# Third mixer's heads issued one by one, four stick-breaking heads in flight, and the conditioning products dealt out anew over the stages

## The chip, the core and the metric

The kernel runs on one core of a Trainium2 chip. The metric is the device time of the whole kernel in microseconds. The kernel before was timed three times: 1038.05, 1036.2 and 1028.79 us, median 1036.2 us. One more execution was recorded by the profiler; it took 1033.1 us, with 1031.4 us from its first to its last instruction.

## The reference, cut to what matters

Three blocks over 256 tokens of width 1024. Each adds a gated mixer and then a gated convolutional FFN to x. Shifts, scales and gates come from the conditioning vector c through a large weight matrix per block; these products are called conditioning products below.

```python
cond = silu(c)
mod = cond @ ada_w[i] + ada_b[i]                 # 1024 x 6144 for each block
sh1, sc1, g1, sh2, sc2, g2 = split(mod, 6)
h = rms_norm(x, norm_mix[i]) * (1.0 + sc1) + sh1
x = x + g1 * mixer_i(h)
h = rms_norm(x, norm_ffn[i]) * (1.0 + sc2) + sh2
x = x + g2 * conv_ffn(h)

# mixer 0, stick-breaking, 16 heads of 64
z = q @ k.T / 8
log_keep = where(strict, log_sigmoid(-z), 0.0)
suffix = cumsum(log_keep, reverse=True) - log_keep
o = where(strict, exp(log_sigmoid(z) + suffix), 0.0) @ v
...
# mixer 1: sparse attention, 64 selected keys a query
...
# mixer 2: 8 heads of sliding-window attention with sinks beside a 4-head recurrence
p = exp(scores - m) / (sum(exp(scores - m)) + exp(sink - m))     # window 128
f = lb + (1 - lb) * sigmoid(f_logit)
S_t = diag(f_t) S_{t-1} + (1 - f_t) i_t^T;  o_t = S_t^T q_t
x = x + gate * (concat([rms_norm(attn), rms_norm(rec) * silu(g)]) @ w_out)
```

## The kernel before

**Weight products.** All large matrix products are taken in three parts: a weight piece (`raw`, 128x1024) is split into a high part `wh` by ScalarE (`high`, L409) and a low part `wl` by VectorE (`low`, L421), the activations likewise into `xh` and `xl`, and TensorE adds wh·xh, wh·xl and wl·xh (`three`, all recorded at L300). One piece is 24 matmuls with 256 columns. There are 290 pieces, and their splits are made three pieces ahead.

**Stages.** The stages follow each other: 0 `stick` (mixer 0), 1 `ffn(0)`, 2 `sparse`, 3 `ffn(1)`, 4 `mixed` (mixer 2), 5 `ffn(2)`. Between two stages stands a serial piece. `residual` adds the gated product to x, one 128x256 part at a time on VectorE (L691), writes `xh` and `xl` of the un-normalised x (L687), and sums squares (L714). `opening` then takes the first six pieces (144 matmuls) of the next stage with the un-normalised x, while the norm goes TensorE sums `po<-ones,sq`, VectorE and ScalarE `rs` (L656 to L662), TensorE spread `po<-ident,rs`, ScalarE `rbc`, VectorE `xm` (L772). The `wl` of these six pieces stand in VectorE's queue among this work.

**Heads.** A mixer's heads run in the background of the dense work. `heads_in_flight` is a generator, advanced by `post` (which is called once after each piece) `rate` times a piece. It keeps some heads between `scores` (score matmuls, which take a bank of the accumulators `acc`, four in all) and `middle` (for stick-breaking the suffix sums, for window heads the transposes `flip`). With `pair` = 2 heads are started two at a time. Two heads of a pair have 64-row operands in the upper and the lower half of the array, and `chained` binds the order of their matmuls. `product` takes two heads at once. In `output` the heads that are still open are brought to their middle before the output product (`acc<-oh,wh` and its like) begins, and `st["out"]` is then true.

**Conditioning products.** A product is one VectorE instruction (`ada_op`, L532) over a 128x1024 block of weights with a short read of the accumulator behind it. Four make a group, with a small `mod` addition behind it (L558); there are 36 groups. The first 4 groups are done before the first stage is under way. The blocks after the first 16 pass through a ring of three buffers; POOL issues the load of a block (`ada_load`, L525, 512 KB) when the product three blocks earlier has freed its buffer. `post` spreads the products evenly over a stage's pieces so that `TARGETS[i]` groups are reached by the end of stage i. Before the change the six stages take 6, 7, 5, 6, 6 and 2 groups.

**Order.** A scheduler, which simulates the program, fixes the order of each engine's instructions when the kernel is built. On the chip VectorE, ScalarE and POOL take theirs strictly in that order.

**Recurrence.** The third mixer's recurrence (`level_decay`, `level_scores`, `recurrence`, L1554 to L1640) has eight levels, two at a time: TensorE decays `acc<-lev,gth` and `acc<-lev,gtl`, ScalarE exponentials `X`, VectorE products `X` (L1574), TensorE scores `acc<-X` or `mm<-X` with 64 columns, VectorE `COPY_PREDICATED` into `S` (L1595). It ends in `mixed` behind the dense input pieces, and the output product waits for it.

Of the kernel before, what the change touches and what calls it, by code (L numbers as in the profile page):

```python
# [208 lines left out]
SPR = 1  # L209
QUIET = (4,4,4,4,6,4)  # L210
FE = 0
TARGETS = (10,17,22,28,34,36)

IX = (2,2,2,2,0,0,0,0)
DD = (1,)*16
# [55 lines left out]
class Prog:  # L271
# [187 lines left out]
    def post(self):  # L459
        i = sum(e < self.pos for e in self.ends)  # L460
        start, end = self.ends[i - 1] + QUIET2[i] if i else 0, self.ends[i] - QUIET[i]
        if start <= self.pos <= end and i != 2:
            ops = 4 * (TARGETS[i] - self.ada_i) - (4 - len(self.ada_todo) if self.ada_todo else 0)
            self.ada_credit = min(self.ada_credit, 1) + max(0, ops - self.ada_credit) / (end + 1 - self.pos)
# [20 lines left out]
    def heads_in_flight(self, n, st, ready, scores, middle, product, lag=2, pair=1):  # L485

        st.update(hold=False, out=False, done=0, open=0, ready=0, split=0)
        a = c = 0
        ticks = {}
        while st["done"] < n:  # L490
            can = a < n and not st["hold"] and ready(a) and a - c < (3 - pair if st["out"] else 4 - pair)
            did = False
            if st["done"] + 1 < c and (st["done"] % 4 or not st["split"]):
                product(st["done"])
                st["done"] += 2
                did = True
            if c < a and (a - c >= 2 or not can) and self.tick - ticks[c] >= lag and c - st["done"] < WP:
                middle(c)
                c += 1
                did = True  # L500
            if can:
                scores(a)
                for a in range(a, a + pair):
                    ticks[a] = self.tick
                a += 1
                did = True
            st["open"] = a - c
            yield did
# [834 lines left out]
    def mixed(self):  # L1343
        nc, I = self.nc, self.I
        blocks = ((0, slice(0, 128)), (1, slice(128, 384)))
        with ExitStack() as outer:
# [4 lines left out]
            band_r = sk.tile([128, 384], F32R, name="band")  # L1351
# [39 lines left out]
            ka = sk.tile([128, T], F32, name="ka")  # L1391
            va = sk.tile([128, 2, 128], F32, name="va")
            st, part = {}, []
            sp = pool("hgx", 2)
            qa = sp.tile([128, 4, T], F32, name="ro")
# [35 lines left out]
            for half in range(2):  # L1431
                h, l = self.next()
# [10 lines left out]
            def keys():  # L1443
                nc.scalar.activation(ka, bkv[:, 0:T], AF.Identity, bias=self.v("bka"))
                nc.vector.tensor_tensor(va, bkv[:, 256:512].rearrange("p (t c) -> p t c", t=2),
                                        rows[:, None, 512:640].to_broadcast([128, 2, 128]), op=ALU.add)
                self.bg.extend([self.heads_in_flight(8, st, lambda h: True, scores, flip, product, 2, 2), window()])

            Z, E, P, PO = {}, {}, {}, {}

            def scores(h0):
                for h in (h0, h0 + 1):
                    Z[h] = self.bank("acc")
                chain = []
                for t, j in ((1, 1), (1, 0), (0, 1), (0, 0)):
                    r = slice(j * 64, j * 64 + 64)
                    chain.append(self.mmul(Z[h0 + j][:, t * 128:128 + t * 256], qa[r, h0 // 2, t * 128:t * 128 + 128],
                                           ka[r, 0:128 + t * 128], start=t == 1))
                self.chained(chain)
                for h in (h0, h0 + 1):  # L1460
                    self.mmul(Z[h][:, 0:384], self.ident_r, band_r, stop=True)
                    softmax(h)

            def softmax(h):
                i, kv = divmod(h, 2)
                z = Z[h]
                sink = self.v("sink", i + 4 * kv, 1)
                m = sp.tile([128, 4, 2], F32, name="wm", bufs=3)
                e = E[h] = sp.tile([128, 384], F32, name="we", bufs=3)
# [265 lines left out]
```

## Time and profile before

| | before |
|---|---|
| three runs, us | 1038.05, 1036.2, 1028.79 (median 1036.2) |
| the profiled execution, us | 1033.1 |
| its span, us | 1031.4 |
| TensorE matmul busy | 998.2 us, 97% |
| VectorE busy | 833.5 us, 81% |
| ScalarE busy | 636.4 us, 62% |
| POOL busy | 98.9 us, 10% |
| mean granted TensorE clock | 0.979 of full speed |

The span is that of the one core from its first to its last instruction. The matmul busy time counts matmuls that are pipelined and whose ends are modelled, so 97% is no measure of TensorE at its peak: at half the granted clock it reads as busy too. The places to read are therefore the stretches in which the clock is below full or in which TensorE waits for something.

### The profile page before, as it was taken

The numbers are of one execution on the slowest core, as the hardware profiler recorded it, in microseconds if no ns is written. First come the engines' busy times: TensorE is split into PE (matmuls) and PEld (weight loads), VectorE is DVE, ScalarE is ACT, GpSimd is POOL, SyncE is SP. The second block draws the span as 40 slices with busy tenths as digits, with TensorE's granted clock in tenths as the row PEclk, the third lists the DMA queues.
The fourth block names the chain that finished last, engine by engine and source line by source line (L and its number), as shares of the span: only waits on it lengthen the run. The fifth ranks groups of instructions, "written<-read, shape, count | busy, mean of one in ns | idle before, by whom it ended". The sixth has DMA issues, their size and how long they took to land.

```text
span 1031.4 us, 19958 instructions
## 1 busy us (share of the span) xinstructions
PE 998.2 (97%) x7984; PEld 964.1 (93%) x7984; DVE 833.5 (81%) x1550; ACT 636.4 (62%) x1095; POOL 98.9 (10%) x180
## 2 busy tenths in 40 slices
PE   7999989999999999998999999999999999999996
PEld 5998878999999989988999999999899999999996
DVE  6956768999999889987998889897994588566664
ACT  6575647855555684886965555588854378445543
POOL 0015530011111010110000101100120000000000
PEclk9999989999999999999999999999986999999998
DMA  9969764578888476642767777745880336566531
GB/s 362 405 239 336 243 241 159 209 276 300 290 295 289 142 275 216 241 169 83 268 225 268 283 268 284 277 150 210 306 312 21 124 127 226 200 210 220 211 137 42
DMA packets 45647, 235.66 MB, mean 228 GB/s; under 512 B 5361, under 2 KB 5889, under 8 KB 27889
## 3 DMA queue, kind: packets, MB, share of 16 engines
q1 hardware_dynamic: 25922, 164.21, 44.1%
q0 software_dynamic: 19344, 69.78, 19.3%
q8 instruction: 62, 1.02, 0.4%
q10 hardware_dynamic: 288, 0.39, 0.1%
q14 instruction: 31, 0.25, 0.1%
HBM read 233.29 MB, written 1.07 MB: 227 GB/s over the span
## 4 chain that ended last, share of the span: by engine, by line
PE 81%; issue 8%; DVE 5%; DMA 3%; ACT 2%; POOL 1%; DVEq 0%; SPq 0%; POOLq 0%; ACTq 0%
PE acc L300 32%; PE mm L300 29%; PE po L300 10%; PE small L300 10%; DMA adaw<-ada 2%; DVE x L691 1%; DVE xl L687 1%; POOL adaw L525 1%; DVE wl L421 1%; DVE adaw L532 1%; ACT wh L409 0%; DMA x<-xT 0%; DVE sq L714 0%; PE acc L1126 0%; ACT e L330 0%
## 5 line engine op out<-in xcount | busy, mean ns | idle before, releaser
L409 ACT ACTIVATE wh<-raw 128x1024 fp32r<-128x1024 f32 x290 | 304.7, 1057 | 224.8 <-PE acc L300 87.1
L421 DVE TENSOR_TENSOR wl<-raw,wh 128x1024 fp32r<-128x1024 f32 x290 | 353.0, 1223 | 96.1 <-PE acc L300 27.8
L300 PE MATMUL mm<-xh,wh 128*128 128x256 f32 (+1 forms) x872 | 244.5, 285 | 2.1 <-ACT wh L409 2.1
L300 PE MATMUL mm<-xl,wh 128*128 128x256 f32 (+1 forms) x872 | 245.4, 283 | 0.7 <-DVE xl L687 0.7
L300 PE MATMUL mm<-xh,wl 128*128 128x256 f32 (+1 forms) x872 | 244.3, 282 | 0.0
L532 DVE SCALAR_TENSOR_TENSOR adaw<-adaw,cond 128x1024 f32<-128x1024 f32 x144 | 175.2, 1221 | 10.7 <-DMA adaw<-ada 10.4
L300 PEld LDWEIGHTS mm<-xh,wh 128*128 128x128 f32 x872 | 163.5, 189 | 4.9 <-ACT wh L409 2.7
L300 PEld LDWEIGHTS mm<-xl,wh 128*128 128x128 f32 x872 | 164.6, 189 | 2.3 <-DVE xl L687 1.1
L300 PEld LDWEIGHTS mm<-xh,wl 128*128 128x128 f32 x872 | 164.0, 188 | 0.5 <-issue 0.3
L300 PE MATMUL acc<-gh,wl 128*128 128x256 f32 x528 | 149.0, 283 | 0.0
L300 PE MATMUL acc<-gh,wh 128*128 128x256 f32 x528 | 148.1, 282 | 0.0
L300 PE MATMUL acc<-gl,wh 128*128 128x256 f32 x528 | 147.9, 281 | 0.0
L525 POOL DMA_DIRECT2D adaw<-ada x125 | 66.6, 533 | 738.6 <-DVE adaw L532 624.9
L300 PEld LDWEIGHTS acc<-gl,wh 128*128 128x128 f32 x528 | 100.3, 190 | 0.2 <-DVE gl L337 0.2
L300 PEld LDWEIGHTS acc<-gh,wh 128*128 128x128 f32 x528 | 98.8, 188 | 0.0
L300 PEld LDWEIGHTS acc<-gh,wl 128*128 128x128 f32 x528 | 98.8, 187 | 0.0
L300 PE MATMUL small<-xh,wh 128*128 128x256 f32 x240 | 67.6, 282 | 0.0
L300 PE MATMUL small<-xh,wl 128*128 128x256 f32 x240 | 67.5, 281 | 0.0
L300 PE MATMUL small<-xl,wh 128*128 128x256 f32 x240 | 67.3, 281 | 0.0
L300 PE MATMUL acc<-oh,wh 128*128 128x256 f32 x192 | 53.1, 297 | 2.0 <-ACT oh L336 1.5
L300 PE MATMUL acc<-xh,wl 128*128 128x258 f32 (+1 forms) x192 | 52.4, 284 | 2.1 <-DVE wl L421 2.0
L300 PE MATMUL acc<-ol,wh 128*128 128x256 f32 x192 | 53.7, 286 | 0.4 <-DVE ol L337 0.4
(310 smaller groups left out, 2073.9 us busy)
## 6 DMA issues: line engine op xcount, KB each, us to landing
raw<-ffn SPq DMA_DIRECT2D x99, 1024.0 KB, 5.0
adaw<-ada POOLq DMA_DIRECT2D x125, 512.0 KB, 5.2
raw<-dsa SPq DMA_DIRECT2D x15, 1024.0 KB, 6.4
raw<-hg SPq DMA_DIRECT2D x15, 1024.0 KB, 5.9
adaw<-ada SPq DMA_DIRECT2D x19, 512.0 KB, 10.2
raw<-sb SPq DMA_DIRECT2D x16, 512.0 KB, 10.2
raw<-sb SPq DMA_DIRECT2D x8, 1024.0 KB, 8.5
bias<-scr POOLq DMA_DIRECT2D x8, 256.0 KB, 8.3
```

What stands on the lines that cost most here:

```text
L300: return self.nc.tensor.matmul(o, a, b, start=start, stop=stop, skip_group_check=True).ins
L409: inst = nc.scalar.activation(h[:, :k * n], self.raws[b][:, c0:c0 + k * n], AF.Copy).ins
L421: inst = nc.vector.tensor_tensor(l[:, :k * n], self.raws[b][:, c0:c0 + k * n], h[:, :k * n], op=ALU.subtract).ins
L525: self.nc.gpsimd.dma_start(raw, self.I[f"ada{L}"][b])
L532: return self.nc.vector.scalar_tensor_tensor(w, w, 1.0, self.cond[n // 24], op0=ALU.mult, op1=ALU.mult, accum_out=self.M[n // 12][:, n % 1 ...
L687: return lambda: nc.vector.scalar_tensor_tensor(self.xl[:, m, 0:T], self.x[:, m], a, self.xh[:, m, 0:T], op0=ALU.mult, op1=ALU.subtract)
L691: self.lastx = nc.vector.scalar_tensor_tensor(self.x[:, m], o, self.gate(L, h, m), self.x[:, m], op0=ALU.mult, op1=ALU.add).ins
```

## The change

Three edits.

1. `TARGETS` goes from (10,17,22,28,34,36) to (13,20,25,32,34,36). The six stages then take 9, 7, 5, 7, 2 and 2 groups: three groups (12 products, 12 loads) more in stage 0, one more in stage 3, four fewer in stage 4.
2. The limit on heads between scores and middle is 3 in place of 4 - `pair` outside of the output product. For `pair` = 1 it stays 3. For stick-breaking (`pair` = 2) it was 2, so that a pair was started only with at most one head waiting; now one is started with two waiting, which makes four heads.
3. The window heads of the third mixer are started singly (`pair` = 1, `lag` = 2 by default). `scores` of one head is a 128-column matmul, a 256-column matmul and the band; nothing is bound by `chained`. `softmax` becomes part of `scores`; lines below move up by nine.

```diff
-TARGETS = (10,17,22,28,34,36)
+TARGETS = (13,20,25,32,34,36)
...
-            can = a < n and not st["hold"] and ready(a) and a - c < (3 - pair if st["out"] else 4 - pair)
+            can = a < n and not st["hold"] and ready(a) and a - c < ((3 - pair) if st["out"] else 3)
...
-                self.bg.extend([self.heads_in_flight(8, st, lambda h: True, scores, flip, product, 2, 2), window()])
+                self.bg.extend([self.heads_in_flight(8, st, lambda h: True, scores, flip, product), window()])
...
-            def scores(h0):
-                for h in (h0, h0 + 1):
-                    Z[h] = self.bank("acc")
-                chain = []
-                for t, j in ((1, 1), (1, 0), (0, 1), (0, 0)):
-                    r = slice(j * 64, j * 64 + 64)
-                    chain.append(self.mmul(Z[h0 + j][:, t * 128:128 + t * 256], qa[r, h0 // 2, t * 128:t * 128 + 128],
-                                           ka[r, 0:128 + t * 128], start=t == 1))
-                self.chained(chain)
-                for h in (h0, h0 + 1):
-                    self.mmul(Z[h][:, 0:384], self.ident_r, band_r, stop=True)
-                    softmax(h)
-
-            def softmax(h):
+            def scores(h):
                 i, kv = divmod(h, 2)
-                z = Z[h]
+                r = slice(kv * 64, kv * 64 + 64)
+                z = Z[h] = self.bank("acc")
+                self.mmul(z[:, 0:128], qa[r, i, 0:128], ka[r, 0:128], start=True)
+                self.mmul(z[:, 128:384], qa[r, i, 128:256], ka[r, :])
+                self.mmul(z[:, 0:384], self.ident_r, band_r, stop=True)
```

**VectorE, between stage 0 and ffn(0).** The names are those of `residual` and `opening` above. Before, from the first `wl` behind the residual to `xm`:

```order
L421 TENSOR_TENSOR wl<-raw,wh 128x1024
L687 SCALAR_TENSOR_TENSOR xl<-x,gain_173,xh 128x256 x3
L714 TENSOR_TENSOR sq<-sq 128x512
L687 SCALAR_TENSOR_TENSOR xl<-x,gain_173,xh 128x256
L421 TENSOR_TENSOR wl<-raw,wh 128x1024
L714 TENSOR_TENSOR sq<-sq 128x512
L656 TENSOR_SCALAR rs_1725<-po 128x2
L659 SCALAR_TENSOR_TENSOR rs_1725<-rs_1725 128x2
L660 TENSOR_TENSOR rs_1725<-rs_1725 128x2
L662 SCALAR_TENSOR_TENSOR rs_1725<-rs_1725 128x2
L421 TENSOR_TENSOR wl<-raw,wh 128x1024
L772 TENSOR_TENSOR xm<-x,po 128x512 x2
```

Of the change, first from the same `wl` to the second one:

```order
L421 TENSOR_TENSOR wl<-raw,wh 128x1024
L532 SCALAR_TENSOR_TENSOR adaw,mod_170<-adaw,cond_167 128x1024
L687 SCALAR_TENSOR_TENSOR xl<-x,gain_173,xh 128x256 x2
L532 SCALAR_TENSOR_TENSOR adaw,mod_170<-adaw,cond_167 128x1024
L687 SCALAR_TENSOR_TENSOR xl<-x,gain_173,xh 128x256
L714 TENSOR_TENSOR sq<-sq 128x512
L532 SCALAR_TENSOR_TENSOR adaw,mod_170<-adaw,cond_167 128x1024
L687 SCALAR_TENSOR_TENSOR xl<-x,gain_173,xh 128x256
L421 TENSOR_TENSOR wl<-raw,wh 128x1024
```

and then, without a gap, on to `xm`:

```order
L714 TENSOR_TENSOR sq<-sq 128x512
L532 SCALAR_TENSOR_TENSOR adaw,mod_171<-adaw,cond_167 128x1024
L558 TENSOR_TENSOR mod_170<-mod_170,vec 128x4
L532 SCALAR_TENSOR_TENSOR adaw,mod_171<-adaw,cond_167 128x1024
L656 TENSOR_SCALAR rs_1765<-po 128x2
L532 SCALAR_TENSOR_TENSOR adaw,mod_171<-adaw,cond_167 128x1024
L659 SCALAR_TENSOR_TENSOR rs_1765<-rs_1765 128x2
L660 TENSOR_TENSOR rs_1765<-rs_1765 128x2
L662 SCALAR_TENSOR_TENSOR rs_1765<-rs_1765 128x2
L421 TENSOR_TENSOR wl<-raw,wh 128x1024
L532 SCALAR_TENSOR_TENSOR adaw,mod_171<-adaw,cond_167 128x1024
L772 TENSOR_TENSOR xm<-x,po 128x512 x2
```

Seven conditioning products (`adaw`) now stand between that `wl` and `xm`, where none stood, and one more stands ahead of that `wl`, between two `x` additions of the residual: eight between the residual's first `x` and `xm`. Of these, four stand ahead of the last `sq`, two between it and the first `rs`, one between two `rs`, and one ahead of `xm`. A ninth stands just ahead of the first `x`.

**TensorE, window heads of the third mixer.** `ka` and `ro` are the keys and queries of the window heads, `band` the mask, `pT` and `va` the weights and values, `mm` dense work. Before, the third pair (one of its matmuls comes ahead of two heads' product):

```order
L300 MATMUL acc<-ka,ro 128x256
L300 MATMUL mm<-wl,xh 128x256
L300 MATMUL po<-pT,va 64x256 x2
L300 MATMUL po<-pT,va 64x128 x2
L300 MATMUL acc<-ka,ro 128x256
L300 MATMUL acc<-ka,ro 128x128 x2
L300 MATMUL acc<-band,ident_r 128x384 x2
```

Of the change, two single heads behind the first product:

```order
L300 MATMUL po<-pT,va 64x256 x2
L300 MATMUL po<-pT,va 64x128 x2
L300 MATMUL acc<-ka,ro 128x128
L300 MATMUL acc<-ka,ro 128x256
L300 MATMUL acc<-band,ident_r 128x384
L1126 MATMUL acc<-ident,we 128x128 x3
L300 MATMUL acc<-ka,ro 128x128
L300 MATMUL acc<-ka,ro 128x256
L300 MATMUL acc<-band,ident_r 128x384
```

A head's three matmuls now stand together, with another head's transposes between two heads, and no two matmuls of different row halves are neighbours. The first two pairs of before stand undivided, the last two are divided as the one shown.

**VectorE, the recurrence's first levels.** `X` and `S` are the recurrence's. Before:

```order
L532 SCALAR_TENSOR_TENSOR adaw,mod_172<-adaw,cond_168 128x1024
L1574 TENSOR_TENSOR X<-X,kq 128x256 x2
L561 SCALAR_TENSOR_TENSOR gain_175<-mod_172,vec 128x2
L421 TENSOR_TENSOR wl<-raw,wh 128x1024
L1574 TENSOR_TENSOR X<-X,kq 128x256 x4
L532 SCALAR_TENSOR_TENSOR adaw,mod_172<-adaw,cond_168 128x1024
L1574 TENSOR_TENSOR X<-X,kq 128x256 x3
L532 SCALAR_TENSOR_TENSOR adaw,mod_172<-adaw,cond_168 128x1024
L1574 TENSOR_TENSOR X<-X,kq 128x256
L1512 TENSOR_TENSOR sq<-sq 128x512
L532 SCALAR_TENSOR_TENSOR adaw,mod_172<-adaw,cond_168 128x1024
L1574 TENSOR_TENSOR X<-X,kq 128x256
```

and of the change, from the start of `S` to the first copy into it:

```order
L1596 TENSOR_TENSOR S<-acc,ident 128x512 x2
L421 TENSOR_TENSOR wl<-raw,wh 128x1024
L1565 TENSOR_TENSOR X<-X,kq 128x256 x7
L1503 TENSOR_TENSOR sq<-sq 128x512
L1565 TENSOR_TENSOR X<-X,kq 128x256 x3
L421 TENSOR_TENSOR wl<-raw,wh 128x1024
L532 SCALAR_TENSOR_TENSOR adaw,mod_172<-adaw,cond_168 128x1024
L1586 COPY_PREDICATED S<-pick,acc 128x512
```

Between the start of `S` and its last copy stood seven products; one is left, behind a `wl` and right ahead of the first copy.

## Rows read from the trace of the kernel before

**Rows 1.** The page of the profile: the span, and the chain of work that ended last, by engine.

```profile
span 1031.4 us, 19958 instructions
...
PE 81%; issue 8%; DVE 5%; DMA 3%; ACT 2%; POOL 1%; DVEq 0%; SPq 0%; POOLq 0%; ACTq 0%
```

**Rows 2.** Busy time by stretch of the span: start and end in us, length, then for PE, PEld, DVE, ACT and POOL the busy us with the count of instructions, the mean granted clock, the DMA engines' share, and GB/s.

```profile
100.00:151.00 51.00, 44.07 (x320) 37.69 (x319) 36.18 (x69) 25.42 (x55) 24.64 (x42) 0.93 0.76 254
151.00:163.00 12.00, 9.80 (x79) 9.34 (x78) 10.60 (x22) 7.57 (x15) 0.00 (x0) 1.00 0.10 39
163.00:176.00 13.00, 13.00 (x111) 13.00 (x110) 11.03 (x21) 11.46 (x21) 0.00 (x0) 1.00 0.67 238
704.00:756.00 52.00, 50.76 (x414) 47.37 (x414) 46.17 (x101) 42.01 (x97) 8.50 (x16) 1.00 0.75 278
756.00:787.00 31.00, 29.07 (x165) 27.98 (x164) 24.03 (x56) 15.46 (x38) 3.18 (x6) 0.66 0.50 175
787.00:807.00 20.00, 19.37 (x127) 18.84 (x127) 6.33 (x13) 7.29 (x21) 0.00 (x0) 0.76 0.00 1
```

**Rows 3.** The same stretches, with the conditioning products and their loads alone: busy us of DVE (a product and its accumulator read count as two) and of POOL.

```profile
100.00:151.00 51.00, 21.41 (x36) 9.69 (x18) 0.93 0.76 254
151.00:163.00 12.00, 0.00 (x0) 0.00 (x0) 1.00 0.10 39
704.00:756.00 52.00, 20.05 (x33) 8.50 (x16) 1.00 0.75 278
756.00:787.00 31.00, 6.76 (x12) 3.18 (x6) 0.66 0.50 175
```

**Rows 4.** The conditioning products from 99 to 151 us: ns of one (min, median, max), first and last start, shape; what they waited for in us and times; and from issue to landing of a load.

```profile
L532 DVE SCALAR_TENSOR_TENSOR adaw<-adaw,cond x18: 1212/1224/1410, 99.0 to 141.2; 128x1024 f32<-128x1024 f32 x18
L532 DVE DVE_READ_ACCUMULATOR adaw<-adaw,cond x18: 75/80/83, 100.2 to 142.3; 128x1 f32 x18
...
  DMA adaw<-ada: 6.8, 5
...
DMA to landing us min/median/max: 3.8/5.0/7.1
```

**Rows 5.** VectorE in order of time, from the residual of stage 0 through the opening of ffn(0): start, us, line, operation; in brackets the idle time before and what ended it.

```profile
150.97 1.66 DVE L691 SCALAR_TENSOR_TENSOR x<-acc,mod,x 128x256 f32<-128x256 f32 x4 [0.62 <-PE acc L300]
...
160.76 0.68 DVE L714 TENSOR_TENSOR sq<-sq 128x512 f32<-128x512 f32 x1
162.64 0.16 DVE L656 TENSOR_SCALAR rs<-po 128x2 f32<-128x2 f32 x1 [1.21 <-PE po L300]
163.31 0.16 DVE L659 SCALAR_TENSOR_TENSOR rs<-rs 128x2 f32<-128x2 f32 x1 [0.51 <-ACT rs L330]
...
165.40 1.28 DVE L772 TENSOR_TENSOR xm<-x,po 128x512 f32<-128x512 f32 x2 [0.41 <-ACT rbc L749]
...
167.74 1.22 DVE L421 TENSOR_TENSOR wl<-raw,wh 128x1024 fp32r<-128x1024 f32 x1
```

**Rows 6.** TensorE in order of time in the end of stage 0 and the opening of ffn(0).

```profile
138.43 0.87 PE L300 MATMUL po<-a,V 128*64 128x256 f32 x8 [1.58 <-POOL a L1031]
...
143.69 1.22 PE L300 MATMUL mm<-s,nu 128*128 128x256 f32 x2 [0.86 <-POOL s L1031]
...
161.58 1.02 PE L300 MATMUL po<-ones,sq 128*128 128x1 f32 x8 [0.71 <-DVE sq L714]
...
164.34 0.61 PE L300 MATMUL po<-ident,rs 128*128 128x128 f32 x4
...
170.53 0.41 PE L300 MATMUL acc<-xh,wl 128*128 128x258 f32 x2
```

**Rows 7.** TensorE in order of time, window heads of the third mixer: the first pair with its bands and the dense matmul behind them, then the third and the beginning of the fourth pair.

```profile
707.11 0.92 PE L300 MATMUL acc<-ka,ro 64*128 64x256 f32 x8
...
708.42 0.28 PE L300 MATMUL mm<-xh,wh 128*128 128x256 f32 x1
...
726.03 0.70 PE L300 MATMUL acc<-ka,ro 64*128 64x256 f32 x2
...
727.78 0.92 PE L300 MATMUL acc<-ka,ro 64*128 64x256 f32 x6
...
729.08 0.28 PE L300 MATMUL mm<-wh,xl 128*128 128x256 f32 x1
...
732.67 0.70 PE L300 MATMUL acc<-ka,ro 64*128 64x256 f32 x2 [0.76 <-ACT pT L1129]
733.84 0.55 PE L1126 MATMUL acc<-ident,we 128*128 128x128 f32 x3 [0.48 <-ACT we L1485]
```

**Rows 8.** TensorE in order of time, the recurrence.

```profile
764.26 0.66 PE L300 MATMUL acc<-X 128*128 128x64 f32 x4 [0.52 <-DVE X L1574]
765.39 0.39 PE L300 MATMUL acc<-lev,gth 128*128 128x256 f32 x1 [0.47 <-ACT X L330]
...
783.22 3.68 PE L300 MATMUL mm<-X 128*128 128x64 f32 x16 [0.78 <-DVE S L1595]
...
787.71 0.58 PE L300 MATMUL mm<-lev,gth 128*128 128x256 f32 x1
...
789.59 0.32 PE L300 MATMUL acc<-ol,wh 128*128 128x256 f32 x1
...
793.76 6.46 PE L300 MATMUL mm<-X 128*128 128x64 f32 x40 [0.63 <-ACT X L330]
```

## The prediction

> **What bounds the kernel now.** I read the page first. Of a span of 1031.4 us the chain that ended last runs 81% through TensorE, 8% through issue, 5% through VectorE and 3% through DMA [rows 1]. Most stages are dense matmuls, so work that moves there between other engines costs nothing while VectorE keeps up. What can change is where TensorE waits or runs at half its clock, so I went on to the busy times by stretch [rows 2]. Two places stand out. From 100 to 163 us (end of the stick-breaking stage, residual, opening of the first FFN) TensorE is busy 53.9 of 63 us. From 756 to 807 us (the recurrence) it reads as busy, but its granted clock is 0.66 and 0.76 of full. The clock has two levels, 1.2 and 2.4 GHz; 0.66 over 31 us makes 2 x 0.34 x 31 = 21.1 us at the lower, 0.76 over 20 us makes 9.6, together 30.7 us. Next I asked where the conditioning products stand [rows 3]: 18 between 100 and 151 us, none from 151 to 176 us, some 16 from 704 to 756, 6 from 756 to 787.
>
> The change takes products away from the second place and puts them into the first. So the sum is made of these two, and of the window heads.
>
> **Stage 0.** Twelve products more must go through the ring. In the end of this stage the ring is already the pace: a product takes 1.224 us and its accumulator read 0.080, together 1.30, but from the first at 99.0 to the eighteenth at 141.2 they come every 2.48 us, and five times VectorE waited for the load, 5.0 us from issue to landing [rows 4]. Leaving out the two longest steps, where nothing asked for a product, I take 2.43. TensorE's own waits in this stretch (for example 1.58 and 0.86 us [rows 6], both for POOL, which also issues the loads) are what four heads in flight could remove. But by the new order 21 further products stand between the one at 99.0 and the first addition to x: the last of them starts at 99.0 + 21 x 2.43 = 150.0, ends at 151.3, and the addition follows, where it came at 150.97 before [rows 5]. So I count no gain from the fourth head, and +0.4.
>
> Then come the eight products between the first x and xm. All three wl and the norm wait behind them in one queue, so I replay that queue with the durations of [rows 5]. Four products stand ahead of the last sum of squares: 160.76 + 5.2 = 165.96. Two products and a mod addition follow: rs, which came at 162.64 after 1.21 us of idle time, comes at 165.96 + 0.68 + 2.6 + 0.07 = 169.3. The seventh covers ScalarE's 0.51: the second rs is at 170.7 instead of 163.31, +7.4. The spread on TensorE, at 164.34 [rows 6], moves by as much, but four dense matmuls (0.5 us) now stand ahead of it, so TensorE loses 6.9. The eighth covers the 0.41 ahead of xm, which comes at 173.75, and the fourth wl at 176.1 instead of 167.74; it ends at 177.3, and TensorE wants it at 170.53 + 6.9 = 177.4 [rows 6], just in time. The seventh and eighth wait for loads issued after the fourth and fifth: 0.5 of issue, 5.0 of landing and 1.30 of product come to about 1 us more than the queue leaves them. That makes 7.9. It isn't given back: behind the opening TensorE is dense, 13.00 of 13.00 us [rows 2].
>
> TensorE's clock: the drain already lost 0.07 of 51 us, that is 7.1 us at the lower level or 3.6 us of work [rows 2]. In the opening TensorE will now wait four or five times in 15 us. The cost lies between 0 and a second such 3.6; I take 1.0, since TensorE waited there before (9.80 busy of 12 us) at full clock. Stage 0 in all: 0.4 + 7.9 + 1.0 = +9.3. Bounds: if loads land as the quickest did, 3.8 us, the pace is about 2.0, x is bound by TensorE, some 3 us earlier, the extra load wait is gone, and +3.9 is left; with a pace 0.1 us longer, 2 us of load waits and the whole clock loss it is 0.4 + 2.1 + 6.9 + 2.0 + 3.6 = +15.
>
> The Trainium skill, "DMA: Bandwidth & Descriptors", Anatomy of one DMA, fits a load issued by GpSimd as 2.0 us plus bytes at 436 GB/s; as an estimate by that page, 512 KB take 3.2 us. The trace's quickest is 3.8 and its median 5.0, so the trace does not agree under this load, and I go by the trace; by the page the ring would turn in about 1.8 us a product and stage 0 would cost what the lower bound says.
>
> **Other stages.** The group added to stage 3 (four products, 5.2 us of VectorE spread over a whole stage of dense pieces) is hidden by dense matmuls; if VectorE were full there, it would cost those 5.2. The sixteen taken from stage 4 free VectorE between 704 and 756 us, where TensorE is busy 50.76 of 52 us [rows 2]: at most 1.2 us, which I count below.
>
> **Window heads singly.** An undivided pair takes 708.42 - 707.11 = 1.31 us with its bands; a divided one 0.70 at 726.03 and 1.30 from 727.78 to 729.08, 2.0 [rows 7]. A single head has no row; I bound it by half an undivided pair (0.66) and half a divided one (1.0), and take 1.0, since nothing in the other row half runs beside it. Two pairs were undivided: 2 x (2.0 - 1.31) = +1.4; the other two gain nothing. Two waits of the fourth pair (0.76 and 0.48 [rows 7]) come from softmax steps that now start a head earlier: -1.2. Net +0.2, from -1.2 to +1.4.
>
> The Trainium skill, "TensorEngine Tiling (Array Packing)", Theoretical Speedup, promises up to twice the throughput where the contraction is 64 or less, and speaks against this edit. By that rule alone all four pairs would lose, four times 0.7, +2.8. The trace agrees for the undivided pairs only; half of the pairs had been pulled apart by the scheduler already.
>
> **Recurrence.** Six products from 756 to 787 us [rows 3], 1.30 us each, stood between its VectorE steps; one is left. TensorE's waits that lead back to those are 0.52, 0.47 and 0.78, and 0.63 before the last scores [rows 8]; also the eight decay matmuls from 787.71 to 789.59 (1.9 us at half clock), which stood behind the first output matmuls, now stand ahead in time that was waited. That sums to 4.3, and the fewer waits in a row give a little of the clock back: -4.5. The clock decides how much more. All 30.7 us at half clock would shrink by 15.4 if it stayed up; a replay of ScalarE's and VectorE's queues by their durations leaves 13.5 of it. Before the fall at about 766 us TensorE had only waits of 0.5 us or so, and in the new order the first copy into S stands behind a wl and a product (2.5 us), so a wait of 1.5 to 1.9 us stands at the same place. I take it that the clock falls again: -4.5, bounds 0 and -13.5.
>
> **Sum.** 9.3 + 0.2 - 4.5 = +5.0 us against the profiled execution's 1033.1 us, 1038.1. The median of the three runs is 3.1 higher than that execution, which would make 1041; I give 1040. About 1% (10 us) is what a measurement of this kernel can tell from no change.
>
> **Rivals.**
> *The clock stays up in the recurrence.* For it: six products leave, and S starts before the decays. Against: the wait at the first copy. It gives 9.3 + 0.2 - 13.5 = -4.0, 1029 to 1032, and is over 1% faster (the other side) only if stage 0 costs less than 3 us, near its lower bound: 1033.1 + 3 - 13.5 = 1022.6. Chance 0.25, of which 0.1 below 1026.
> *The ring is quick enough.* Loads land in less than 4 us, the stage is bound by its heads, and four in flight save TensorE's waits there. For it: the quickest load, and the DMA share of 0.10 from 151 to 163 us [rows 2]. Against: a share of 0.76 before. It gives 3.9 + 0.2 - 4.5: no change, 1033 to 1036. Chance 0.15. The fit of the Trainium skill's page named above would make this case the likeliest; no load of this ring in the trace was as quick as it says.
> *The clock falls in the opening as well, or the loads are late there.* Stage 0 at +13 to +15, and in the recurrence half the gain: +11 to +13, 1046 to 1050. Chance 0.2.
> *The change does little:* pairs that were mostly divided, and heads that wait for VectorE with or without a fourth; that is part of the sum above and has no price of its own.
>
> **Chances.** Likeliest 0.4, at 1040 with its own range 1035 to 1045; the others as above. The range 1028 to 1051 takes in all but the low end of the first rival and the high end of the third. Faster by over 1%: 0.14; slower by over 1%, above 1046.5: 0.22 (the third rival and the top of the likeliest); within: 0.64.
>
> **What would show it.** In the profile after, eight conditioning products between the first x and xm, xm about 22 us after the first x (it was 14.4), and TensorE waiting 6 to 8 us more there than the 2.2 it did. Products every 2.4 us up to the first x, at about 151. Window heads at 1.0 us each. In the recurrence at most one product, and a granted clock still below full from about 764 us. I am wrong if xm follows x as before, if the drain of the heads ends by 147 us, or if the recurrence's clock reads 1.00.

## The result, and the profile after

The change makes the kernel faster, by little: 1026.05 us in the median of 20 runs (1023.58 to 1028.81) against 1031.8 us of the kernel before in 20 runs (1028.45 to 1038.05). The ratio is 0.9938, 95% interval 0.9924 to 0.9952: 6 us, inside the 1% that was called no change, but of the other sign than forecast and below the stated range. The profiled execution took 1026.6 us, its span is 1024.9 us.

Two things have to be kept apart. The time of before was taken as 1036.2 us, the median of three runs; 20 runs put it at 1031.8. And the sum was made against one profiled execution, whose mean granted clock was 0.979; in the 83 further runs of before that came with the experiments the mean clock lies between 0.971 and 0.989, 0.984 in the median, and the time follows it (correlation 0.85 between a run's time and its time multiplied by one minus its clock). The changed kernel's 20 runs lie between 0.987 and 0.992, 0.990 in the median. A run's time multiplied by its mean clock is 1014.9 us for before and 1015.4 us for the changed kernel, its time multiplied by one minus the clock 16.5 and 10.3 us (medians over the runs; before's are over the 83). So the difference between the kernels is about as large as the difference in what the lower clock took. This is a rough measure, since it counts a low clock as lost also where TensorE would have waited otherwise: in the changed kernel's profile (1 - 0.70) x 22.7 = 6.8 us of it stand between the first addition to x and xm in the first opening, where they cost no time that shows (see the part on stage 0).

Where the two traces differ, stretch by stretch, for the changed kernel. The columns are as in [rows 2].

```profile
100.00:151.00 51.00, 42.74 (x328) 36.82 (x326) 42.78 (x82) 26.11 (x57) 29.47 (x46) 1.00 0.79 276
151.00:163.00 12.00, 8.40 (x53) 7.98 (x53) 12.00 (x25) 6.85 (x13) 1.71 (x4) 0.80 0.60 214
163.00:176.00 13.00, 12.19 (x72) 11.92 (x72) 11.79 (x21) 4.70 (x10) 2.53 (x5) 0.66 0.81 268
704.00:756.00 52.00, 52.00 (x404) 47.46 (x404) 35.29 (x75) 42.41 (x95) 2.12 (x4) 1.00 0.50 181
756.00:787.00 31.00, 30.30 (x259) 29.03 (x258) 25.05 (x52) 21.85 (x54) 1.58 (x3) 1.00 0.44 154
787.00:807.00 20.00, 19.01 (x159) 18.68 (x160) 10.20 (x22) 9.03 (x23) 0.53 (x1) 1.00 0.03 5
```

The clock has changed places. In the recurrence it is 1.00, where [rows 2] had 0.66 and 0.76; from 151 to 176 us it is 0.80 and 0.66, where it had 1.00. VectorE is now full from 151 to 163 us (12.00 of 12).

The opening of the first FFN on VectorE, in order of time, to be read against [rows 5]:

```profile
148.45 1.22 DVE L532 SCALAR_TENSOR_TENSOR adaw<-adaw,cond 128x1024 f32<-128x1024 f32 x1 [1.02 <-DMA adaw<-ada]
...
149.60 1.26 DVE L691 SCALAR_TENSOR_TENSOR x<-acc,mod,x 128x256 f32<-128x256 f32 x3
...
164.04 0.69 DVE L714 TENSOR_TENSOR sq<-sq 128x512 f32<-128x512 f32 x1
164.64 1.22 DVE L532 SCALAR_TENSOR_TENSOR adaw<-adaw,cond 128x1024 f32<-128x1024 f32 x1
...
165.86 1.22 DVE L532 SCALAR_TENSOR_TENSOR adaw<-adaw,cond 128x1024 f32<-128x1024 f32 x1
...
167.00 0.15 DVE L656 TENSOR_SCALAR rs<-po 128x2 f32<-128x2 f32 x1
167.73 1.23 DVE L532 SCALAR_TENSOR_TENSOR adaw<-adaw,cond 128x1024 f32<-128x1024 f32 x1 [0.57 <-DMA adaw<-ada]
...
168.88 0.16 DVE L659 SCALAR_TENSOR_TENSOR rs<-rs 128x2 f32<-128x2 f32 x1
...
170.76 1.22 DVE L532 SCALAR_TENSOR_TENSOR adaw<-adaw,cond 128x1024 f32<-128x1024 f32 x1 [0.20 <-DMA adaw<-ada]
...
172.31 1.28 DVE L772 TENSOR_TENSOR xm<-x,po 128x512 f32<-128x512 f32 x2 [0.32 <-ACT rbc L749]
```

From the first x to xm it is 172.31 - 149.60 = 22.7 us (14.4 before): the eight products stand in the chain, and the idle times of 1.21 and 0.51 us in [rows 5] are gone into them. The first x is 1.4 us earlier than before, right behind the product that starts at 148.45.

The stretches of the whole kernel, from the starts of the first residual addition (x) and the first xm of each stage in the traces, in us:

| stretch | before | after | difference |
|---|---|---|---|
| start to first x of stage 0 | 151.0 | 149.6 | -1.4 |
| that x to xm | 14.4 | 22.7 | +8.3 |
| first FFN, xm to the next x | 177.9 | 177.5 | -0.4 |
| opening, sparse mixer, opening, second FFN | 325.5 | 326.4 | +0.9 |
| opening of the third mixer | 14.0 | 15.5 | +1.5 |
| third mixer, xm to the next x | 141.7 | 126.7 | -15.0 |
| the rest | 207.0 | 206.5 | -0.5 |

In the third mixer the first decay matmul comes 0.9 us later after xm (73.9, was 73.0), from it to the start of the last score matmul it takes 30.6 us (was 44.1), and from there to the x 22.1 (was 24.6).

### The profile page after: what moved, and what is told of

Read it like the earlier page. It is cut to its first block, busy times and chain, and to the rows that moved or that the text cites. A ratio compares the mean times of both kernels' runs of the same rounds, so it can differ in the third digit from the quotient of the medians.

```text
span 1024.9 us, 19967 instructions
## 1 busy us (share of the span) xinstructions
PE 990.4 (97%) x7984; PEld 956.5 (93%) x7984; DVE 833.8 (81%) x1550; ACT 636.5 (62%) x1095; POOL 102.9 (10%) x180
## 4 chain that ended last, share of the span: by engine, by line
PE 87%; DVE 6%; ACT 2%; DMA 2%; issue 1%; POOL 1%; DVEq 0%; SPq 0%; POOLq 0%; ACTq 0%
PE acc L300 34%; PE mm L300 32%; PE po L300 10%; PE small L300 10%; DMA adaw<-ada 2%; DVE adaw L532 1%; DVE x L691 1%; DVE xl L687 1%; DVE wl L421 1%; ACT wh L409 1%; PE acc L1126 1%; DVE sq L714 0%; DMA x<-xT 0%; POOL s L1031 0%; POOL a L1031 0%
## 5 line engine op out<-in xcount | busy, mean ns | idle before, releaser
L421 DVE TENSOR_TENSOR wl<-raw,wh 128x1024 fp32r<-128x1024 f32 x290 | 352.8, 1223 | 103.3 <-PE acc L300 30.6
L300 PE MATMUL acc<-gh,wh 128*128 128x256 f32 x528 | 147.9, 282 | 0.0
L300 PE MATMUL acc<-xh,wh 128*128 128x258 f32 (+1 forms) x192 | 55.6, 298 | 0.0
```

The costliest lines, as they stand in the source:

```text
L300: return self.nc.tensor.matmul(o, a, b, start=start, stop=stop, skip_group_check=True).ins
L421: inst = nc.vector.tensor_tensor(l[:, :k * n], self.raws[b][:, c0:c0 + k * n], h[:, :k * n], op=ALU.subtract).ins
```

## The experiments

The table puts the runs together: the median, the ratio to before with its interval as recorded (not the ratio of the medians shown), the median of the runs' mean clocks (for before: of the 83), and of the profile the first x of stage 0, the stretch from it to xm, the third mixer from xm to x, and the granted clock from 755 to 807 us.

| kernel | us | ratio | clock of the runs | first x | x to xm | mixer | recurrence |
|---|---|---|---|---|---|---|---|
| before (profile shown) | 1031.8 | | 0.984 | 151.0 | 14.4 | 141.7 | 0.70 |
| before again | 1031.68 | 0.9998 (0.997 to 1.0025) | 0.984 | 152.3 | 14.5 | 139.6 | 0.84 |
| the change | 1026.05 | 0.9938 (0.9924 to 0.9952) | 0.990 | 149.6 | 22.7 | 126.7 | 1.00 |
| TARGETS alone | 1029.67 | 0.9987 (0.9966 to 1.0008) | 0.985 | 150.2 | 23.7 | 125.5 | 1.00 |
| single heads alone | 1030.73 | 1.0004 (0.9969 to 1.0039) | 0.985 | 152.2 | 15.3 | 133.1 | 0.97 |
| limit alone | 1025.63 | 0.9951 (0.9928 to 0.9975) | 0.989 | 145.3 | 14.4 | 140.1 | 0.84 |
| both edits on heads | 1026.12 | 0.9925 (0.9892 to 0.9958) | 0.990 | 145.6 | 14.5 | 141.8 | 0.74 |
| change, 10 groups in the first FFN | 1023.8 | 0.9915 (0.9884 to 0.9946) | 0.992 | 145.8 | 14.4 | 127.8 | 0.97 |
| change, groups spread | 1020.78 | 0.9875 (0.9843 to 0.9907) | 0.992 | 147.6 | 14.5 | 129.5 | 0.93 |
| the same again | 1021.18 | 0.9889 (0.985 to 0.9928) | 0.992 | 147.9 | 15.3 | 126.6 | 1.00 |
| spread, one group in stage 0 | 1021.35 | 0.9889 (0.9846 to 0.9933) | 0.992 | 149.5 | 14.5 | 128.2 | 0.97 |
| spread, matmuls added | 1019.9 | 0.987 (0.9818 to 0.9921) | 0.994 | 148.3 | 14.4 | 127.3 | 1.00 |
| before, matmuls added | 1026.18 | 0.9937 (0.991 to 0.9963) | 0.992 | 151.0 | 14.5 | 133.7 | 0.97 |
| change, VectorE operations added | 1030.86 | 0.9982 (0.9956 to 1.0007) | 0.986 | 149.6 | 22.7 | 129.3 | 1.00 |

**TARGETS alone.**

```diff
-TARGETS = (10,17,22,28,34,36)
+TARGETS = (13,20,25,32,34,36)
```

> The kernel before with the new TARGETS alone. In its order seven products stand between the first x and xm of the first opening, and one in the recurrence. Theory A (the products leaving the recurrence keep the clock up there, and that is the gain): xm of the first opening 6 to 8 us later, the recurrence at a granted clock of 1.00 and 12 to 14 us shorter, the whole -5 to -7 us. Rival B (the single heads bring the gain, by an earlier and lighter recurrence): the recurrence's clock falls as before, its gain is at most 4 us, the whole +2 to +5 us.

In the profile theory A holds in the main: xm of the first opening is 8.5 us later (150.2 + 23.7 against 165.4), a little over its 6 to 8, the recurrence is at full clock, the mixer 16.2 us shorter. The two stretches from 100 to 176 and from 755 to 807 us:

```profile
100.00:176.00 76.00, 61.99 (x429) 55.54 (x429) 65.43 (x123) 35.92 (x75) 28.39 (x53) 0.89 0.77 268
755.00:807.00 52.00, 48.94 (x415) 47.32 (x414) 35.86 (x75) 31.54 (x77) 2.12 (x4) 1.00 0.26 94
```

The whole does not: 2.4 us in the medians, which the interval cannot tell from nothing. The profiled execution, 1026.75 us with a mean clock of 0.988, was the fastest of its ten, whose clocks have a median of 0.985; before's, with 0.979, was below the median of 0.984. One profile of each says where a loss can stand, not how often it does.

**Single heads alone.**

```diff
-            self.bg.extend([self.heads_in_flight(8, st, lambda h: True, scores, flip, product, 2, 2), window()])
+            self.bg.extend([self.heads_in_flight(8, st, lambda h: True, scores, flip, product), window()])
```

with the new `scores`, and everything else as before.

> The kernel before with the window heads singly, alone. Five products stand in the recurrence in place of seven. Theory A: the clock falls in the recurrence as before, the whole 0 to -4 us. Rival B: the recurrence's clock is 1.00, the whole -12 to -15 us, since nothing is paid in the first opening.

No difference in the medians, as theory A had it at the edge, and rival B falls. In the profile the recurrence read 0.97, against theory A; the runs' mean clocks go from 0.973 to 0.989, as wide as before's, so the single heads do not keep the clock up in general.

**Limit alone.**

```diff
-            can = a < n and not st["hold"] and ready(a) and a - c < (3 - pair if st["out"] else 4 - pair)
+            can = a < n and not st["hold"] and ready(a) and a - c < ((3 - pair) if st["out"] else 3)
```

> The kernel before with the new limit on heads alone, which acts on the stick-breaking heads. Theory A: the first x of stage 0 moves by less than 1.5 us, as the products' ring paces it, the whole within 2 us. Rival C (the fourth head saves the waits in the drain): the first x 3 us or more earlier than at 151.0, the whole -3 us or more.

Rival C holds, with 5.7 us at the first x and a ratio of 0.9951 in the whole. Without products behind it the residual begins as soon as the heads are done:

```profile
145.33 1.66 DVE L691 SCALAR_TENSOR_TENSOR x<-acc,mod,x 128x256 f32<-128x256 f32 x4 [0.61 <-PE acc L300]
```

The clock from 100 to 176 us is 1.00 in this profile (0.96 in before's), and the one edit is worth as much as the whole change.

**The change with stage 0 as before, the first FFN with ten groups.**

```diff
-TARGETS = (13,20,25,32,34,36)
+TARGETS = (10,20,25,32,34,36)
```

> The changed kernel with TARGETS (10,20,25,32,34,36): stage 0 keeps its 6 groups, and the three that it took go to the first FFN, which has 10. No product stands between the first x and xm of the first opening, one in the recurrence. Theory A: the mixer's gain of 15 us stays and stage 0 pays nothing: -13 to -16 us against before, about 1017 us. Rival D (the FFN stage has no room on VectorE for three groups more): the first FFN 3 us or more longer than the 177.9 us from xm to the first x that it had, the whole -8 to -12 us.

Rival D holds. The mixer keeps its gain (127.8) and the first x comes at 145.8, but the first FFN takes 186.4 us instead of 177.9. TensorE in order of time there:

```profile
326.71 0.73 PE L300 MATMUL acc<-gh,wh 128*128 128x256 f32 x4 [1.55 <-ACT gh L336]
330.92 0.58 PE L300 MATMUL acc<-gl,wh 128*128 128x256 f32 x1 [3.48 <-DVE gl L337]
```

The longer wait is for VectorE, which was busy 23.1 of 26 us there, and around these waits the clock is at its lower level for a while (0.87 from 320 to 346 us).

**Both edits on heads, with the TARGETS of before.**

```diff
-TARGETS = (13,20,25,32,34,36)
+TARGETS = (10,17,22,28,34,36)
```

> The changed kernel with the TARGETS of before: the edits on heads alone (four stick-breaking heads in flight, window heads singly). No product stands in the first opening, five in the recurrence in place of seven. Theory A (the parts add up as they measured alone): first x of stage 0 at about 145.5 as with the limit alone, mixer about 133 us from xm to the next first x as with the single heads alone (141.7 before), the whole -12 to -14 us in the profiled run. Rival F (the clock of the recurrence decides by chance of the order): the recurrence falls to half clock again, mixer 138 us or more, the whole -5 to -8 us.

Stage 0 is as theory A had it, the mixer as rival F. With five products in it the recurrence falls to half clock again in the profiled execution, which had a mean clock of 0.984 where the median of the six runs is 0.990:

```profile
756.00:787.00 31.00, 27.84 (x144) 26.97 (x143) 21.34 (x49) 13.39 (x36) 2.65 (x5) 0.59 0.46 160
```

This kernel differs from the changed one in TARGETS alone and has the same median (1026.12 and 1026.05): on top of the edits on heads, the groups moved by the change bring nothing. In the two profiles they gain 15.1 us in the mixer (126.7 against 141.8), and xm of the first opening comes 12.3 us later (172.3 against 160.0).

**Before once more.** No edit.

> The kernel before once more, run by run, with its clock. Theory A (the half-clock stretch of the recurrence belongs to this order of instructions): the profiled run again has a granted clock of 0.6 to 0.8 between 756 and 807 us, and the runs' mean clocks lie near 0.979. Rival F (it falls only in some executions): the mean clocks range up to 0.99, and the runs with the higher clock are the shorter ones, 10 us or more apart.

Both hold in part. The recurrence was below full clock again, but over another part of it:

```profile
755.00:807.00 52.00, 45.26 (x317) 43.16 (x316) 32.71 (x73) 24.00 (x60) 3.70 (x7) 0.84 0.38 137
```

The twelve runs go from 1027.82 us at 0.986 to 1040.96 us at 0.978 (lowest clock 0.973, highest 0.987). So the fall in the recurrence came in both profiles of this order of instructions, but neither its place nor its length is fixed.

**Matmuls added to before.** Ahead of the scores of levels 0, 1 and 2:

```diff
                 n = 64 // half
+                if e in (0, 1, 2):
+                    for i in range(12):
+                        self.mmul(p[:, 0:256], gh[:, i % 2, i % 4], lev[:, 0:2], start=True)
```

> The kernel before with 36 dense matmuls added in the recurrence: ahead of the score matmuls of its first three levels twelve decay matmuls each into the bank that the scores then write anew (at full clock 0.119 us each, together 4.3 us). Nothing is taken away. Theory A (the loss in the recurrence is the clock, which falls because TensorE's work there is thin): the clock stays at 1.00 from 756 to 807 us, the recurrence saves 12 to 15 us and pays 4.3, the mixer 8 to 11 us shorter. Rival G (the loss is the wait for VectorE's products): the mixer is 2 to 5 us longer.

More work, and the kernel is 6.4 us faster; the mixer is 8.0 us shorter than in the first profile of before and 5.9 shorter than in the second, with the 4.3 us of added matmuls in it. TensorE in order of time at the first levels, and the stretch:

```profile
759.65 1.68 PE L300 MATMUL acc<-lev,gth 128*128 128x256 f32 x12
761.17 0.55 PE L300 MATMUL acc<-X 128*128 128x64 f32 x4
...
766.79 1.59 PE L300 MATMUL acc<-lev,gth 128*128 128x256 f32 x12
768.21 1.90 PE L300 MATMUL acc<-X 128*128 128x64 f32 x16
```

```profile
755.00:807.00 52.00, 49.46 (x403) 47.88 (x402) 39.52 (x87) 26.02 (x64) 4.78 (x9) 0.97 0.39 140
```

All seven products still stand in the recurrence. Sixteen score matmuls take 1.90 us here at full clock. So most of the loss there is the clock, not the wait for VectorE as such, and rival G falls.

**VectorE operations added to the change.** Six in the recurrence, four in levels 0 and 1 and two in levels 2 and 3:

```diff
+                        if (e, h) in ((0, 1), (0, 3), (2, 1)):
+                            y = self.x[:, 0:4]
+                            self.behind(nc.vector.tensor_tensor(y, y, y, op=ALU.max).ins, xi)
```

where `xi` is the X product before it.

> The changed kernel with six VectorE operations of the size of a conditioning product (x = max(x, x) on half of x, which leaves x as it is) put back between the X products of the recurrence's first levels. No product moves. Theory A (what stands on VectorE in the recurrence decides whether the clock falls there): a stretch of 10 us or more at half clock between 765 and 800 us in the profile, mixer 136 us or more (126.7 in the changed kernel), the whole +8 to +12 us against the changed kernel, and lower mean clocks. Rival H (only the single heads and the free place of the changed order matter): clock 1.00, mixer at most 131 us, the whole within +4 us.

The profile is rival H's: clock 1.00, mixer 129.3 us, 2.6 longer. The ten runs lie between the two theories: 4.8 us longer than the change, with clocks of 0.983 to 0.985 in five of them, a level that none of the change's 20 runs had (lowest 0.987); time multiplied by clock is 1015.9, as for the change. About half of the runs lost clock, and the profiled one was not among them, so no profile shows in which stretch they lost it. That VectorE's load in the recurrence matters is therefore supported but not shown, and the order that the change made there holds the clock in some runs even with that load.

**Groups spread over the stages.**

```diff
-TARGETS = (13,20,25,32,34,36)
+TARGETS = (10,18,23,31,34,36)
```

> The changed kernel with TARGETS (10,18,23,31,34,36): 6, 8, 5, 8, 3 and 2 groups, so that stage 0 stays free, the FFN stages take one and two more than before, and the mixer three fewer. No product in the first opening, two in the recurrence. Theory A: first x at about 145.5, both FFN stages within 1 us of before (177.9 and 177.7 us from xm to the next first x), mixer 126 to 130 us, the whole -16 to -20 us, about 1014 us. Rival D (VectorE has no room in the FFN stages): the stages with eight groups are 2 to 5 us longer each.

The edits on heads keep their gain, the mixer has three groups instead of six, and the FFN stages pay little (179.1 and 179.2 us from xm to x, 177.9 and 177.6 before), which lies between the two theories. It is the better kernel: 5.3 us faster than the change. The mixer is where theory A put it; the whole gains 11.8 us in the medians, less than forecast, since the first x came 2.1 us later than 145.5 (147.6), the FFN stages paid 2.7 us together, and the openings of the second FFN and of the third mixer took 0.9 and 1.5 us longer in the profile than before's. Run once more:

> The spread kernel (TARGETS (10,18,23,31,34,36)) once more, for its interval. Theory A: 1019 to 1022 us, ratio 0.986 to 0.990 against before, and mean clocks of 0.991 to 0.994. Rival F (the clock in the recurrence is a matter of chance in this order as well): some runs 8 us or more longer with mean clocks below 0.988.

1021.18 us: theory A as to the time. The clocks spread more than it said, from 0.987 to 0.995, with one run of six below 0.988 (1024.68 us at 0.987, 6.5 us over the shortest). In this second profile the FFN stages take 180.8 and 178.8 us.

**One group of these in stage 0.**

```diff
-TARGETS = (10,18,23,31,34,36)
+TARGETS = (11,18,23,31,34,36)
```

> The spread kernel with TARGETS (11,18,23,31,34,36): one group of the first FFN goes to stage 0, which has 7 groups; its order has no product between the first x and xm. Theory A (stage 0 pays for products only where they stand in the opening or where the ring is later than the heads): first x at most 1 us later than the spread kernel's 147.6, the first FFN back at 178 us (179.1), the whole within 1.5 us of it. Rival I (each product in stage 0 costs ring time, 2.4 us): first x 4 to 8 us later, the whole 4 to 8 us longer.

No difference in the whole. The first x is 1.9 us later than in the spread kernel's first profile, the first FFN 1.2 us shorter. Neither theory's number for the first x is met: four more products cost less than 0.5 us each there, far from a ring turn of 2.4. With six groups the last product ahead of x starts at 142.73 in the spread kernel's first profile, and VectorE then waits 1.84 us for ScalarE (oh, a head's output) and 0.62 for TensorE; with seven it starts at 148.31 after 0.69 us of waiting for its load, and x follows right behind it. So with six groups the ring does not bind the end of that stage, and with seven it just does.

**Matmuls added to the spread kernel.** As above, eight each ahead of the scores of levels 1, 2 and 3.

> The spread kernel (TARGETS (10,18,23,31,34,36)) with eight dense matmuls added ahead of the scores of levels 1, 2 and 3 (24, 2.9 us at full clock). Its profile had 6.8 us at half clock at 779.9 us. Theory A: that stretch goes, saving up to 3.4 us for 2.9 paid: within 1 us of the spread kernel in the median, with mean clocks 0.002 higher. Rival G (the loss is the wait for VectorE): 2 to 3 us longer at the same clock.

1019.9 us, within the interval of the spread kernel, at clocks of 0.993 to 0.995 in four runs. Theory A; too close to call a gain.

## Why the prediction was wrong, step by step

**The recurrence: the step that failed.** "I take it that the clock falls again: -4.5" chose the wrong branch. The stretch from the first decay to the last score shrank by 44.1 - 30.6 = 13.5 us, the replay's value for a clock that stays up, and 2.5 us more behind it; the mixer gained 15.0. The ground for the choice was a wait of 1.5 to 1.9 us of TensorE at the first copy into S. It did not come: from 704 us to 786 us the changed kernel has no wait of TensorE above 0.3 us, where decay matmuls filled the time. The first longer one is for ScalarE, 1.60 us at 787.89, and behind it the clock stayed up:

```profile
781.95 3.82 PE L300 MATMUL acc<-X 128*128 128x64 f32 x32
...
787.89 0.74 PE L300 MATMUL acc<-oh,wh 128*128 128x256 f32 x4 [1.60 <-ACT oh L342]
...
791.93 4.63 PE L300 MATMUL mm<-X 128*128 128x64 f32 x40
```

Forty score matmuls in 4.63 us stand here against 6.46 us in [rows 8].

Nor does such a wait decide by itself. In TARGETS alone TensorE did wait 1.33 us for a copy into S, at 783.27, and the clock from 756 to 807 us was 1.00. The spread kernel ran twice with nearly the same wait ahead of the output product; the first line is of its first profile, the second of its second:

```profile
780.78 1.22 PE L300 MATMUL acc<-oh,wh 128*128 128x256 f32 x4 [1.90 <-ACT oh L342]
```

```profile
783.96 0.74 PE L300 MATMUL acc<-oh,wh 128*128 128x256 f32 x4 [1.91 <-ACT oh L342]
```

From 756 to 787 us the clock read 0.89 in the first, where the four matmuls took 1.22 us, and 1.00 in the second, where they took 0.74.

That the loss in before's recurrence is the clock's is shown by the matmuls added to before. That the change keeps the clock up there in its other executions too is an estimate from its 20 runs: 13.5 us lost again would lower a run's mean clock by about 13.5 / 1026 = 0.013, and the lowest of them is 0.987, where the profiled one had 0.989. Which of the parts holds it up is shown only in part: with the products moved the recurrence read 0.93 or more in all eight profiles (one of them with six other operations put back, one with matmuls added), with five to seven products left and nothing added 0.70, 0.84, 0.84, 0.74, and 0.97 once, with the single heads alone. But the runs of TARGETS alone have clocks of 0.982 to 0.988, and its profile was the best of them, so the moved products alone are not shown to hold it in every execution.

**Stage 0: right in its mechanism, mis-sized.** Forecast +9.3, measured xm at 172.3 against 165.4, +6.9. The chain was right: the replay put xm 22.4 us behind the first x, and it came 22.7 us behind it, with load waits of 0.57 and 0.20 us, where 1 us had been added for them. The ring turned in (148.45 - 98.98) / 21 = 2.36 us a product rather than 2.43, which made the first x 1.4 us earlier instead of 0.4 later:

```profile
L532 DVE SCALAR_TENSOR_TENSOR adaw<-adaw,cond x22: 1212/1225/1462, 99.0 to 148.5; 128x1024 f32<-128x1024 f32 x22
...
DMA to landing us min/median/max: 3.9/4.7/7.0
```

The load's median of 4.7 us is far from the 3.2 that, as an estimate, the fit of the Trainium skill, "DMA: Bandwidth & Descriptors", Anatomy of one DMA, makes it; no load of this ring was under 3.9. The clock did fall in the opening, as the third rival had it, and the 1.0 us put down for it did not show. Busy times of before, then of the changed kernel, from the first x to xm and from xm to the next x:

```profile
150.97:165.40 14.43, 12.23 (x100) 11.77 (x99) 12.24 (x26) 9.15 (x18) 0.00 (x0) 1.00 0.08 32
165.40:343.30 177.90, 177.90 (x1492) 177.71 (x1491) 162.19 (x260) 109.59 (x151) 14.86 (x28) 1.00 0.79 278
```

```profile
149.60:172.31 22.71, 17.75 (x97) 17.07 (x98) 21.55 (x46) 9.47 (x18) 4.26 (x9) 0.70 0.67 230
172.31:349.80 177.49, 177.49 (x1488) 177.30 (x1488) 162.20 (x263) 109.56 (x151) 15.31 (x29) 1.00 0.80 282
```

From the first x to xm VectorE is busy 21.55 of 22.71 us, and its queue sets the pace; TensorE does nearly as many matmuls as before (97 and 100), more slowly, and has as many left for the FFN, which is no longer. TensorE's idle time rose by 2.8 us there (4.96 against 2.20), not by the 6 to 8 that the prediction named as a sign: the low clock filled the rest.

**The fourth head.** "So I count no gain from the fourth head" was right for this kernel and hid the most useful fact. Alone the limit gives 5.7 us in stage 0; in the change the ring holds the residual back, 149.6 against 145.3, and takes 4.3 of it. The change's own parts undo each other.

**Window heads.** A single head takes longer than the 1.0 us taken for it:

```profile
716.14 0.92 PE L300 MATMUL acc<-ka,ro 64*128 64x128 f32 x4
716.99 0.44 PE L300 MATMUL acc<-band,ident_r 128*128 128x384 f32 x1
717.36 0.92 PE L300 MATMUL acc<-ka,ro 64*128 64x128 f32 x4
718.21 0.44 PE L300 MATMUL acc<-band,ident_r 128*128 128x384 f32 x1
718.48 0.28 PE L300 MATMUL mm<-xh,wh 128*128 128x256 f32 x1
```

Two in a row take 718.48 - 716.14 = 2.34 us up to the next dense matmul, and a head by itself 1.14 (from 737.09 to 738.23). The eight heads come as two such pairs and four single ones: 2 x 2.34 + 4 x 1.14 = 9.2 us against 2 x 1.31 + 2 x 2.0 = 6.6 before, +2.6 where +1.4 was forecast. The prediction's estimate by the rule of the Trainium skill, "TensorEngine Tiling (Array Packing)", Theoretical Speedup, was +2.8, which is nearer. The waits for pT and we (1.24 us) went, as forecast.

**Later openings.** +0.9 in the second FFN's and +1.5 in the third mixer's were not forecast. The latter has a stretch at half clock (0.5 of full from 687.3 to 690.7 us), which is worth 1.7 us. The spread kernel took 15.5 us for this opening in one execution and 14.2 in the other, and the change with VectorE operations added 14.0, so the 1.5 us belong to the execution.

**The base.** 1.9 us were added to the sum because the median of three runs stood above the profiled execution; over 20 runs that execution is above the median (1033.1 and 1031.8). Against 1031.8 us the same sum would have made 1037.

**The rivals.** The first (the clock stays up in the recurrence, 0.25) and the clock's fall in the opening, from the third (0.2), came together, a pair that no case held. "Within 1%" was the likeliest and came true by luck: in the traces a loss of 7 us in stage 0 stands against a gain of 15 in the mixer, where +9.3 and -4.5 were forecast. The first rival's own working, -4.0 us, came to -6.5 between the two traces: stage 0 cost 2.4 us less and the mixer gained 1.7 more than it said, and the rest of the kernel was 1.5 us longer.

## What to carry to other kernels

Where TensorE's clock falls, try what keeps it fed before what shortens the chain: 36 matmuls whose results are not used gained 6 us here. Work moved off one serial piece should go where the engine has room over a whole stage, not to the next serial piece; three groups spread over two FFN stages made these 2.7 and 4.0 us longer in two profiles, the three put into one of them made it 8.5 us longer, and eight products in one opening made that 8.3 us longer. And before a profile's loss is priced, see how much of it other runs have: the mean clock of each run tells more than one trace does.

## What the runs showed of the hardware that was not expected

TensorE's lower clock moved about between executions of one kernel: before had 0.70 and 0.84 of full from 755 to 807 us in two profiles, and 0.971 to 0.989 over whole runs, which is 0.018 x 1030 = 18.5 us between the ends. And it came down with no wait longer than 0.52 us in sight ([rows 8], ahead of 766 us), at the beginning of 24 score matmuls of 64 columns:

```profile
766.12 5.22 PE L300 MATMUL acc<-X 128*128 128x64 f32 x24
```

Such matmuls alone do not bring it down: in the changed kernel 32 of them in a row ran at full clock (3.82 us at 781.95). With dense matmuls added ahead of them it read 0.97 from 755 to 807 us. What decides between the two levels there, these runs do not show.
